# One encoder block on one core: load queues, load order, and PSUM banks rearranged from mLSTM to the last matmul

## The chip, the cores and the metric

The kernel runs on one core of one Trainium2 chip. The metric is the device time of one execution in microseconds (us). Five engines work side by side, each on its own instruction stream and in order: TensorE (PE, with its weight loads, PEld), VectorE (DVE), ScalarE (ACT), GpSimd (POOL) and SyncE (SP). A DMA is started by an instruction on SP or POOL; a waiting instruction holds up everything behind it on the same engine.

## The reference

The input is x, 1024 rows of 1024 float32 channels, and one layer of parameters.

- xn = rmsnorm(x). One matrix w_in projects it to mLSTM's queries, keys, values, output gate and 16 gate channels, to attention's queries, keys and values, and to two sets of merge gates ga, gb.
- mLSTM: four heads (key width 128, value width 256), in both directions, in chunks of 128 rows. For each chunk, scores are weighted with exp(D - m), with D from cumulated gates; a state C is carried from chunk to chunk. Both directions are added, normalized and gated: h_a.
- Differential attention: eight heads with two softmaxes each (width 64, rope on queries and keys), weights p0 - lam*p1, times values of width 128, normalized: h_b.
- Merge: y = sigmoid(ga)*(h_a @ p_a) + sigmoid(gb)*(h_b @ p_b); x1 = x + y @ w_o.
- ConvFFN: u = rmsnorm(x1) @ w_up (5632 channels), a 3-tap convolution along the rows in each channel with a bias, (gelu(g)*a) @ w_down, added to x1.

## The kernel before

Nearly every product is made of three TensorE matmuls (`mm3`, lines 111 to 113): each float32 operand is split into a rounded high part and a low part (`split`, line 80 on ACT, line 82 on DVE or, in four pieces, line 87 on POOL). A stationary weight block is loaded from DRAM as a raw tile of 128 x 1024 (`Weights.load`, line 207, tag `wraw`, NR = 1 buffer for the whole kernel), split into `whi` and `wlo` (four buffers each), and the raw tile is free again after both. A projection needs two such loads, called g = 0 and 1.

The program is written with pools of tiles. A planner that simulates the kernel with a cost model sets the order of instructions on each engine; semaphores are put where a tile is written, read or reused. `K.mark` (line 703) keeps weight splits behind a given activation.

- **mLSTM** (`mlstm`, lines 257 to 545). Eight x tiles are loaded, in two halves (`load_x`, line 281), normalized and transposed by PE into xn. Then come the projections of head 0 (`project`, with `wqk` and `wv`), the 16 gate channels and a long chain over rows of 36 partitions on ACT and DVE (lines 362 to 414), whose results go through DRAM (u_d, iw_d) and come back broadcast over 128 partitions (pm, qs, lines 448 and 457). `core(h)` turns pm into exp(pm + cT) in eight pieces on ACT (line 451), masks it on POOL (line 453) and multiplies it with the scores on DVE (line 455); qs is multiplied on POOL (line 458), kw on DVE (line 460). Then chunk products run on PE (lines 471 to 476), while `ogate(h)` and `project(h+1)` give PE the other work. At the end of `project`, ACT copies kt (line 322), and `finish(h)` transposes the head's result (line 508).
- **Attention** (`attention`, lines 548 to 890). Thirty-two steps (8 heads x 4 pairs of query blocks). A step has the scores and softmax of the next step (`soft`, lines 697 to 708), the transposes and products of this one (`av`, lines 728 and 746), the end of the last one (`tail2`: scale `og` on ACT, line 766; transposes, line 769; `oT`, line 771; store hb_d, line 772) and a `filler`: projections for a later head or merge gates. `qk_piece` makes the keys and queries of a later head; `qk_turn` transposes them and stores the keys in order with four small DMAs on SP (kst, line 682), on which the scores wait. Fillers start weight loads on SP (line 207); POOL makes their low parts (line 87). The rope tables cos and sin come on SP too (line 630), sin with one buffer that POOL reads. POOL also takes the power -0.5 for norms (line 230).
- **Merge** (`merge_ffn`, lines 893 to 998). The tags are `wk` (2 buffers), `B` (16), `acc` (8) and `A` (16). For p_a, the blocks that are not done in attention are multiplied while `load_hb` brings h_b (hraw, tag `wk`, line 916) and splits it; the gates come in as tgl (tag `wk`, line 939). Then p_b and w_o follow. The convolution's parameters cw and cb are read one float32 at a time from DRAM (lines 1017 and 1018) and used some 270 us later. PSUM is four single banks and two double ones here; before `Up.run` this pool is closed and one of eight single banks is opened.
- **Up** (lines 1001 to 1253) and **Down** (lines 1256 to 1420). w_up's product is done in a seven-product scheme for 22 column blocks, each followed by the convolution, gelu and stores h_d. Down does w_down in seven products n of NK = 11 blocks kk: for each, `make` loads a weight tile wd when n < 2 (line 1300, tag `B` for even and `A` for odd), then `prep` calls `act`, which requests the activations hr (line 1332, tag `acc`, two kk per load), and splits both. Three blocks are made ahead. One block is four row tiles of three matmuls.

## Time and profile before

| what | value |
|---|---|
| times of three runs | 2169.25, 2174.41 (median), 2174.93 us |
| the profiled execution's own time, and its span | 2177.57 and 2175.8 us |
| PE busy (11804 matmuls), weight loads | 2095.0 us, 1809.5 us |
| DVE, ACT, POOL busy | 1297.1, 971.5, 412.4 us |
| mean granted clock of PE | 0.984 |
| DMA moved, mean | 217.38 MB, 100 GB/s |

The stages lie about at 0 to 490 us (mLSTM), 490 to 1265 (attention), 1265 to 1500 (merge) and 1500 to 1946 (Up), and Down is the rest. A busy PE need not be PE at its peak: the granted clock of a stretch must be read beside it, where 1.00 is 2.4 GHz and 0.50 is 1.2 GHz. In a row of instructions the bracket at the end is the time that the engine stood idle before it and what it waited for.

### The profile page before, as it was taken

The page shows a single profiled execution, that of the slowest core. Times are in us where ns is not written, and L with a number is a line of the kernel's source. Part 1 is how long each engine was busy: PE and PEld are TensorE (multiplying, and loading weights), DVE is VectorE, ACT ScalarE, POOL GpSimd, SP SyncE. Part 2 cuts the span into 40 slices and gives each one's busy share as a digit, 9 for nine tenths or more (in the row PEclk, how much of TensorE's full clock was granted, in tenths as well). Part 3 has the DMA queues.
Part 4 walks back from the last instruction along what each step waited for, and adds up shares of the span by engine and source line. Part 5 has one row for each costly group of instructions (what it writes and reads, how often), then busy time and mean ns, then how long its engine had stood idle before and what let it go on. Part 6 is the DMA issues. An engine that isn't in the chain of part 4 may idle for free.

```text
span 2175.8 us, 30577 instructions
## 1 busy us (share of the span) xinstructions
PE 2095.0 (96%) x11804; PEld 1809.5 (83%) x11804; DVE 1297.1 (60%) x2110; ACT 971.5 (45%) x1837; POOL 412.4 (19%) x487
## 2 busy tenths in 40 slices
PE   7999999999999899999999999999999999979999
PEld 6878878898898898988988887898788888868887
DVE  4356343545585766848756424425877777778554
ACT  4343232234565555646655422205645444434443
POOL 0122101132341523414220000000121122120000
PEclk9999999999999999999999999999999999999999
DMA  4224221253322325133332385511232323266441
GB/s 127 39 84 123 67 60 49 68 136 59 100 59 54 84 56 93 53 82 75 78 99 78 127 180 182 160 45 78 87 112 84 121 87 116 91 243 242 139 136 46
DMA packets 210242, 217.38 MB, mean 100 GB/s; under 512 B 40841, under 2 KB 172969, under 8 KB 210097
## 3 DMA queue, kind: packets, MB, share of 16 engines
q1 hardware_dynamic: 202224, 187.58, 30.6%
q0 software_dynamic: 7872, 27.86, 3.8%
q8 instruction: 93, 1.52, 0.3%
q14 instruction: 53, 0.43, 0.1%
HBM read 149.82 MB, written 48.79 MB: 91 GB/s over the span
## 4 chain that ended last, share of the span: by engine, by line
PE 76%; DMA 8%; DVE 5%; ACT 4%; issue 4%; POOL 2%; SPq 1%; ACTq 0%; DVEq 0%; POOLq 0%
PE sm L112 12%; PE sm L113 12%; PE sm L111 12%; PE pj L111 8%; PE pj L113 8%; PE pj L112 8%; DMA wraw<-in_w_in_dram 4%; PE big L697 4%; PE pt L728 1%; DMA kst<-st 1%; PE cr L471 1%; PE po L111 1%; PE po L112 1%; PE po L113 1%; POOL wlo L87 1%
## 5 line engine op out<-in xcount | busy, mean ns | idle before, releaser
L111 PE MATMUL pj<-whi,xn 128*128 128x256 f32 x960 | 274.9, 286 | 1.2 <-ACT raw L624 0.5
L113 PE MATMUL pj<-whi,xn 128*128 128x256 f32 x960 | 274.3, 286 | 0.0
L112 PE MATMUL pj<-wlo,xn 128*128 128x256 f32 x960 | 273.8, 285 | 0.0
L111 PE MATMUL pj<-xn,whi 128*128 128x512 f32 x512 | 211.7, 415 | 3.8 <-ACT xn L252 3.1
L113 PE MATMUL pj<-xn,wlo 128*128 128x512 f32 x512 | 208.3, 407 | 0.0
L112 PE MATMUL pj<-xn,whi 128*128 128x512 f32 x512 | 207.9, 406 | 0.0
L80 ACT CAST whi<-wraw 128x1024 fp32r<-128x1024 f32 x88 | 92.3, 1049 | 226.7 <-DMA wraw<-in_w_in_dram 118.0
L111 PEld LDWEIGHTS pj<-whi,xn 128*128 128x128 f32 x960 | 182.7, 190 | 4.9 <-ACT raw L624 1.0
L112 PEld LDWEIGHTS pj<-wlo,xn 128*128 128x128 f32 x960 | 182.6, 190 | 1.9
L113 PEld LDWEIGHTS pj<-whi,xn 128*128 128x128 f32 x960 | 182.6, 190 | 1.4
L703 ACT ACTIVATE p<-big,smx 128x1024 f32<-128x1024 f32 x128 | 143.5, 1122 | 76.8 <-DVE smx L701 65.2
L701 DVE TENSOR_REDUCE smx<-big 128x1 f32<-128x1024 f32 x128 | 154.3, 1217 | 38.8 <-PE big L697 38.2
L82 DVE TENSOR_TENSOR wlo<-wraw,whi 128x1024 fp32r<-128x1024 f32 x54 | 67.2, 1244 | 181.9 <-ACT whi L80 181.9
L697 PE MATMUL big<-kst,qst 128*128 128x512 f32 x512 | 145.4, 405 | 12.3 <-DMA kst<-st 9.3
L1230 POOL TENSOR_TENSOR cv<-cv,cv 128x256 f32<-128x256 f32 x88 | 78.9, 923 | 355.9 <-ACT cv L1226 134.1
L87 POOL TENSOR_TENSOR wlo<-wraw,whi 128x256 fp32r<-128x256 f32 x136 | 112.2, 856 | 163.6 <-ACT whi L80 163.6
L113 PE MATMUL sm<-AS,ul 128*128 128x512 f32 x352 | 138.6, 397 | 0.9 <-DVE ul L82 0.9
L112 PE MATMUL sm<-AS,uh 128*128 128x512 f32 x352 | 138.6, 395 | 0.9 <-DVE AS L82 0.9
L111 PE MATMUL sm<-AS,uh 128*128 128x512 f32 x352 | 138.3, 395 | 0.4 <-ACT AS L80 0.4
L82 DVE TENSOR_TENSOR wTl<-pt,wTh 128x512 fp32r<-128x512 f32 x128 | 86.5, 685 | 81.1 <-ACT wTh L80 80.9
L111 PE MATMUL sm<-dh 128*128 128x512 f32 x308 | 120.0, 393 | 13.6 <-ACT dh L80 13.6
L111 PEld LDWEIGHTS pj<-xn,whi 128*128 128x128 f32 x512 | 98.6, 193 | 26.7 <-ACT xn L252 3.5
(303 smaller groups left out, 5287.7 us busy)
## 6 DMA issues: line engine op xcount, KB each, us to landing
ur<-in_w_up_dram SPq DMA_DIRECT2D x88, 256.0 KB, 3.4
wraw<-in_w_in_dram SPq DMA_DIRECT2D x40, 512.0 KB, 5.2
hr<-h_d SPq DMA_DIRECT2D x35, 512.0 KB, 6.3
kst<-st SPq DMA_DIRECT2D x128, 128.0 KB, 2.4
wraw<-in_w_in_dram SPq DMA_DIRECT2D x48, 256.0 KB, 4.7
h_d<-cv SPq DMA_DIRECT2D x22, 512.0 KB, 3.2
wd<-in_w_down_dram SPq DMA_DIRECT2D x22, 512.0 KB, 6.3
x<-in_x_dram SPq DMA_DIRECT2D x16, 512.0 KB, 4.6
```

What stands on the lines that cost most here:

```text
L80: self.nc.scalar.copy(hi, src)
L82: self.nc.vector.tensor_tensor(lo, src, hi.bitcast(F32), op=ALU.subtract)
L87: lo_eng.tensor_tensor(lo[:, t], src[:, t], hi[:, t].bitcast(F32), op=ALU.subtract)
L111: mm(ps, a[0], b[0], start=start, stop=False, skip_group_check=again)
L112: mm(ps, a[0], b[1], start=False, stop=False, skip_group_check=again)
L113: mm(ps, a[1], b[0], start=False, stop=stop, skip_group_check=again)
L471: T.matmul(nps[:, :MV + 1], pm[:, t], va[:, j, :], start=True, stop=i == 0)
L697: T.matmul(sps[c_][:, half * 512:half * 512 + 512], o.q[st.qp][:, c_, t], o.k[half][:, c_, s_, :], start=s_ == 0, stop=s_ == 1)
L701: V.tensor_reduce(sm[:, c_:c_ + 1], sp, op=ALU.max, axis=AX.X, negate=True)
L703: K.mark = A.activation(p_, sp, AF.Exp, bias=sm[:, c_:c_ + 1], accum_out=sm[:, 2 + c_:3 + c_]).ins
L728: T.transpose(pt[:, kk * 256 + j * P:kk * 256 + (j + 1) * P], st.w[j][:, kb * P:(kb + 1) * P], K.ident)
L1230: nc.gpsimd.tensor_tensor(a[:, t], a[:, t], g[:, t], op=ALU.mult)
```

## The change

1. Raw weight tiles alternate between two buffers in mLSTM (`rawp`: one of the pool wp, one of mLSTM's own pool).
2. The second half of x is requested after the first half is normalized, on POOL's queue.
3. exp(pm + cT): one DVE addition of 128 x 1024 and one ACT exponential take the place of eight ACT pieces; qs is multiplied on DVE.
4. In attention, from step 1 on, weight loads are issued by POOL (`ldq`), and sin by POOL throughout.
5. `tail2` keeps the scaling; the transposes, oT and the store become `tail3`, called inside the next `av` after its first yield.
6. Merge: PSUM is eight single banks from the start, and there is no second pool; gates for p_a are loaded straight into ya; the convolution's parameters are loaded as rows of 128 (craw, tag `wk`) and transposed by PE (`turn_conv`).
7. Down: `act` is called ahead of the weight load, and the first two hr tiles take tag `B`.

```diff
-    def wgran(self, loads, lo_eng=None):
...
     def load(self, g):
         K = self.K
-        self.raw = K.wp.tile([P, 1024], F32, tag="wraw", bufs=NR, name=K.nm("wraw"))
+        K.nraw += 1
+        self.raw = K.rawp[K.nraw % len(K.rawp)].tile([P, 1024], F32, tag="wraw", bufs=NR, name=K.nm("wraw"))
...
-            K.nc.sync.dma_start(self.raw.rearrange("p (k c) -> p k c", k=4)[:, :, off:off + n],
-                                s[g * 512:(g + 1) * 512].rearrange("(k p) c -> p k c", p=P))
+            (K.ldq or K.nc.sync).dma_start(self.raw.rearrange("p (k c) -> p k c", k=4)[:, :, off:off + n],
+                                           s[g * 512:(g + 1) * 512].rearrange("(k p) c -> p k c", p=P))
...
         K.psum(es, {"pj": 2, "cr": 4}, 1)
+        K.rawp = [K.wp, mp]
...
             if first:
-                xs0 = load_x(0)
+                xs0 = load_x(0, nc.sync)
             wqk = K.load_w([w_in[:, O_MQ + h * 128:O_MQ + h * 128 + 128], w_in[:, O_MK + h * 128:O_MK + h * 128 + 128]])
-            if first:
-                xs1 = load_x(1)
...
             if first:
                 norm(xs0, 0)
+                xs1 = load_x(1, G)
...
-                for j in range(8):
-                    t = slice(j * P, (j + 1) * P)
-                    A.activation(pm[:, t], pm[:, t], AF.Exp, bias=cT[:, j, rr:rr + 1])
+                V.tensor_tensor(ch(pm), ch(pm), bc(cT[:, :, rr:rr + 1], [P, 8, P]), op=ALU.add)
+                A.activation(pm, pm, AF.Exp)
...
-                G.tensor_tensor(qs, qT, qs, op=ALU.mult)
+                V.tensor_tensor(qs, qT, qs, op=ALU.mult)
...
-            for t_, d_ in zip((cos, sin), K.rope_d):
-                nc.sync.dma_start(t_, d_[bp * P:(bp + 1) * P, :])
+            for q_, t_, d_ in zip((nc.sync, G), (cos, sin), K.rope_d):
+                q_.dma_start(t_, d_[bp * P:(bp + 1) * P, :])
...
-        def av(st, hook):
+        def av(st, hook, hook0):
...
                 yield
+                if kp == 0 and hook0:
+                    hook0()
                 if kp < 2:
...
                 A.activation(st.og[:, t], po[:, t], AF.Copy, scale=inv[:, 6 + j:7 + j])
+
+        def tail3(st):
+            po = st.po
             for j in range(2):
...
+            if i == 1:
+                K.ldq = G
...
-            both(av(cur, (lambda: soft(o, nxt, 1)) if nxt else None), filler(h, 2 * qp))
+            both(av(cur, (lambda: soft(o, nxt, 1)) if nxt else None,
+                    (lambda: tail3(steps[i - 1])) if i else None), filler(h, 2 * qp))
...
+        K.ldq = None
...
-        K.psum(es, {"sm": 4})
+        K.psum(es, {"sm": 8}, 0)
...
+        craw = g4("craw", tag="wk")[:NFF * 2, :4 * P]
+        for t in range(4):
+            src = I["conv_w"][0][t, 0] if t < 3 else I["conv_b"][0]
+            nc.sync.dma_start(craw[:, t * P:(t + 1) * P], src.rearrange("(k p) -> k p", p=P))
+        conv = fp.tile([P, 3, 44], F32, tag="cw", name="cw"), fp.tile([P, 44], F32, tag="cb", name="cb")
+
+        def turn_conv():
+            ps = K.small()
+            for t in range(4):
+                T.transpose(ps[:, t * 44:t * 44 + 44], craw[:, t * P:(t + 1) * P], K.ident[:44, :44])
+            V.tensor_copy(conv[0].rearrange("p t k -> p (t k)"), ps[:, :132])
+            V.tensor_copy(conv[1], ps[:, 132:176])
...
-                    tg = g4("tgl", tag="wk")
+                    tg = g4("tgl", tag="wk") if gidx else ya[m]
...
                         if gidx == 0:
+                            if m == K.ny + 1 and half == 0:
+                                turn_conv()
...
-        up.norm0([g4("nxs", tag="wk") for _ in range(2)] + [g4("nxs", tag="B") for _ in range(2)], pair)
+        up.norm0([g4("nxs", tag="wk") for _ in range(2)] + [g4("nxs", tag="B") for _ in range(2)], lambda k: K.small())
...
-        es.close()
-        K.psum(es, {"sm": 8}, 0)
         up.run()
...
-        for t in range(3):
-            nc.sync.dma_start(self.cw[:, t, :], K.I["conv_w"][0][t, 0].rearrange("(k p) -> p k", p=P))
-        nc.sync.dma_start(self.cb, K.I["conv_b"][0].rearrange("(k p) -> p k", p=P))
+        self.cw, self.cb = conv
...
-        if kk % 2 == 0:
+        if kk % 2 == 0 and (n, kk) not in self.raw:
             (i, c), m = self.ORDER[n][0], min(2, self.NK - kk)
-            t = self.g4("hr", tag="acc")
+            t = self.g4("hr", tag="B" if n == 0 and kk < 4 else "acc")
...
         def make(n, kk):
+            self.act(n, kk)
             if n < 2:
                 self.load_w(kk * 2 + n)
```

## Rows read from the trace of the kernel before

**Rows 1.** PE's waits: engine, line, waited for: us in total, times, longest us
```profile
PE sm L111 <- ACT dh L80: 13.6, 1, 13.6
...
PE big L697 <- DMA kst<-st: 9.3, 5, 4.1
PE cr L508 <- ACT kt L322: 7.2, 2, 5.3
...
PE po L769 <- ACT og L766: 4.3, 2, 2.3
...
PE pj L111 <- ACT xn L252: 3.1, 1, 3.1
PE sm L111 <- ACT f L1074: 3.0, 1, 3.0
```

**Rows 2.** Stretches: us, busy us of PE, PEld, DVE, ACT, POOL, clock, DMA share, GB/s
```profile
97.00:136.00 39.00, 32.64 (x148) 26.05 (x147) 30.00 (x34) 16.86 (x40) 15.23 (x16) 0.87 0.39 117
278.00:290.00 12.00, 6.70 (x34) 5.94 (x34) 6.14 (x7) 2.51 (x4) 0.00 (x0) 0.72 0.59 100
655.00:668.00 13.00, 8.89 (x53) 8.39 (x52) 5.10 (x11) 6.44 (x16) 4.00 (x5) 0.74 0.47 100
748.00:760.00 12.00, 7.86 (x30) 6.10 (x29) 4.55 (x9) 6.11 (x15) 3.65 (x5) 0.72 0.56 120
935.00:945.00 10.00, 7.99 (x33) 6.05 (x32) 4.84 (x9) 4.29 (x12) 3.35 (x5) 0.83 0.33 95
1106.00:1116.00 10.00, 7.71 (x32) 5.91 (x31) 5.10 (x9) 4.62 (x10) 3.84 (x6) 0.83 0.35 83
1311.00:1328.00 17.00, 11.95 (x35) 8.48 (x34) 7.36 (x8) 5.03 (x5) 2.36 (x5) 0.70 0.57 185
1503.00:1515.00 12.00, 9.00 (x41) 7.10 (x40) 7.64 (x14) 7.92 (x14) 1.65 (x2) 0.86 0.23 88
1944.00:1966.00 22.00, 8.39 (x27) 6.33 (x26) 17.18 (x24) 8.90 (x13) 4.24 (x5) 0.69 1.02 393
2000.00:2050.00 50.00, 50.00 (x222) 41.42 (x221) 29.43 (x47) 21.27 (x38) 0.00 (x0) 1.00 0.29 91
```

**Rows 3.** ACT in order of time at the start: start us, us, instruction [idle before]
```profile
14.72 1.04 ACT L80 CAST whi<-wraw 128x1024 fp32r<-128x1024 f32 x1 [3.37 <-DMA wraw<-in_w_in_dram]
15.98 1.03 ACT L242 ACTIVATE big<-x 128x1024 f32<-128x1024 f32 x1 [0.22 <-DMA x<-in_x_dram]
```

**Rows 4.** ACT and DVE in order of time, 85 to 132 us
```profile
87.70 1.05 ACT L80 CAST whi<-wraw 128x1024 fp32r<-128x1024 f32 x1 [5.58 <-DMA wraw<-in_w_in_dram]
...
121.88 6.41 DVE L460 TENSOR_TENSOR kw<-kt,e1T 128x1024 f32<-128x1024 f32 x2 [4.32 <-ACT e1T L421]
```

**Rows 5.** ACT in order of time, 255 to 300 us
```profile
282.78 1.04 ACT L80 CAST whi<-wraw 128x1024 fp32r<-128x1024 f32 x1 [7.11 <-DMA wraw<-in_w_in_dram]
```

**Rows 6.** SP's issues in order of time, 640 to 664 us
```profile
654.51 0.94 SPq L207 DMA_DIRECT2D wraw<-in_w_in_dram  x2
655.54 2.56 SPq L682 DMA_DIRECT2D kst<-st  x4
```

**Rows 7.** SP's waits in attention, 495 to 1200 us
```profile
SPq L207 <- POOL wlo L87: 82.0, 26, 4.8
```

**Rows 8.** POOL by line: busy us, mean ns, idle before; triggers (all), powers (490 to 1250)
```profile
L448 POOL DMA_DIRECT2D pm<-u_d x8 | 4.6, 578 | 4.1 <-DVE dn L486 2.8 <-DMA u_d<-row 1.2
...
L230 POOL TENSOR_TENSOR inv<-inv,mhalf 128x2 f32<-128x2 f32 x31 | 23.6, 760 | 274.1 <-DVE inv L229 274.0
```

**Rows 9.** SP's issues in order of time, 1195 to 1330 us
```profile
1272.71 13.73 SPq L1017 DMA_DIRECT2D cw<-in_conv_w_dram  x3
...
1291.35 35.41 SPq L207 DMA_DIRECT2D wraw<-in_p_b_dram  x5
```

**Rows 10.** Chain that ended last, in order of time, 1940 to 1965 us
```profile
1946.06 0.02 issue
...
1947.94 11.02 DMA hr<-h_d
```

More of the change, by code (lines that the diff above doesn't have):

```diff
@@ L61, in __init__ @@
         self.gst, self.ng, self.ny = {}, 0, 0
+        self.rawp, self.nraw, self.ldq = [self.wp], 0, None
     def nm(self, s):
@@ L87, in split @@
             lo_eng.tensor_tensor(lo[:, t], src[:, t], hi[:, t].bitcast(F32), op=ALU.subtract)
-    def wgran(self, loads, lo_eng=None):
-        nc = self.nc
-        raw = self.wp.tile([P, 1024], F32, tag="wraw", bufs=NR, name=self.nm("wraw"))
-        for view, src in loads:
-            nc.sync.dma_start(view(raw), src)
-        hi = self.wp.tile([P, 1024], F32R, tag="whi", bufs=NH, name=self.nm("whi"))
-        lo = self.wp.tile([P, 1024], F32R, tag="wlo", bufs=NW, name=self.nm("wlo"))
-        self.split(hi, lo, raw, lo_eng)
-        return hi, lo
     def load_w(self, srcs, lo_eng=None):
@@ L274, in mlstm, with load_x @@
         xv = I["x"][0]
-        def load_x(half):
+        def load_x(half, eng):
             r = []
@@ L280, in load_x @@
                 t = mp.tile([P, 1024], F32, tag="r4", bufs=9, name=K.nm("x"))
-                nc.sync.dma_start(t, xv[blk * P:(blk + 1) * P, :])
+                eng.dma_start(t, xv[blk * P:(blk + 1) * P, :])
                 r.append(t)
@@ L545, in mlstm @@
             finish(h, hs, t1)
+        K.rawp = [K.wp]
 def attention(K, xn, hb_d):
@@ L890, in attention @@
         tail2(steps[-1])
+        tail3(steps[-1])
 def merge_ffn(K, ha_d, hb_d, out):
@@ L960, in merge_ffn @@
         nc.sync.dma_start(g2, I["norm2"][0].rearrange("(k p) -> p k", p=P))
-        pw = []
-        def pair(k):
-            if k % 2 == 0:
-                pw.append(K.big())
-            return pw[-1][:, k % 2 * 512:k % 2 * 512 + 512]
         def wo_piece(w, cg, b0):
@@ L984, in merge_ffn @@
         ws = [wo(2), wo(3)]
-        up = Up(K, g4, acc, g2, fp)
+        up = Up(K, g4, acc, g2, fp, conv)
         up.us = [up.load(0), up.load(1)]
@@ L1001, with __init__ @@
 class Up:
-    def __init__(self, K, g4, acc, g2, fp):
+    def __init__(self, K, g4, acc, g2, fp, conv):
         self.K, self.g4, self.acc, self.g2 = K, g4, acc, g2
@@ L1013, in __init__ @@
         nc = K.nc
-        self.cw = fp.tile([P, 3, 44], F32, tag="cw", name="cw")
-        self.cb = fp.tile([P, 44], F32, tag="cb", name="cb")
-        for t in range(3):
-            nc.sync.dma_start(self.cw[:, t, :], K.I["conv_w"][0][t, 0].rearrange("(k p) -> p k", p=P))
-        nc.sync.dma_start(self.cb, K.I["conv_b"][0].rearrange("(k p) -> p k", p=P))
+        self.cw, self.cb = conv
         self.x1_d = K.dr.tile([S, D], F32, tag="x1_d", name="x1_d")
@@ L1333, in act @@
                                      src.rearrange("(k p) t -> p k t", p=P))
-            self.raw[n] = t
-        return self.raw[n][:, kk % 2 * 512:kk % 2 * 512 + 512]
+            self.raw[n, kk] = t
+        return self.raw[n, kk // 2 * 2][:, kk % 2 * 512:kk % 2 * 512 + 512]
     def prep(self, n, kk):
```

## The prediction, made before the result was known

> **What bounds the kernel now.** First PE's busy time: 2095.0 of 2175.8 us. PE never stops for long, so a change that leaves PE's matmuls as they are can win back only two things: the time in which PE waits, and the time in which it runs at the low clock after a wait. So the second view is the list of PE's waits [rows 1]: the reader is to see that they are few and long (13.6 us once, 9.3 in five, 7.2 in two), and that each has a place. The third view takes a stretch around each place [rows 2] and gives two numbers: the length less PE's busy time is idle, and the mean clock c says how much of the stretch was granted 1.2 instead of 2.4 GHz: 2(1-c) of its length, since there are only these two levels. Work done then takes twice as long, so the clock costs at most (1-c) times the length; a part of the low stretch is the wait itself, so I take two thirds. Around 2000 us the clock is 1.00 and 222 matmuls fill 50 us: 0.225 us each at full pace.
>
> Idle plus clock, in us: 97 to 136: 6.4 + 3.4 = 9.8. 278 to 290: 5.3 + 2.2 = 7.5. 655 to 668: 4.1 + 2.3 = 6.4. 748 to 760: 4.1 + 2.2 = 6.3. 935 to 945: 2.0 + 1.1 = 3.1. 1106 to 1116: 2.3 + 1.1 = 3.4. 1311 to 1328: 5.1 + 3.4 = 8.5. 1503 to 1515: 3.0 + 1.1 = 4.1. 1944 to 1966 holds one kind of matmul, so it goes directly: 22 - 27 x 0.225 = 15.9. Outside these: 3.1 at the start and 1.9 (7.2 - 5.3) for the second of the L508 waits [rows 1]. The sum is 70 us. The change touches each of these places, so 70 us is what it can win from them.
>
> **Part by part.** *Start.* ACT runs in order; at 14 us it holds the weight cast until 14.72, then a square over x's second half until 17, and only then the first xn copy on which PE waits 3.1 us [rows 1, 3]. With that half of x asked for after the first norm, neither stands in the way. PE needs the second half only after the first half's products. Bounds: -3.1 to +1 (one square's length late); I take -2.5, near the wait's own size.
>
> *Second raw buffer.* ACT waited 5.6 us at 82 to 87.7 for a weight load that could start only when the one buffer was free; the gate rows come behind it on ACT, and their chain ends in both PE waits of 97 to 136 [rows 2, 4]. At 275.7 the same: 7.1 us of waiting ahead of the kt copy that PE's transposes need [rows 1, 5]. With two buffers the second load of a pair travels beside the first, so the chain starts up to 5.6 us earlier, against 6.4 us of idle in it. What is late next is pm on DVE, behind two kw's that took 6.41 us together beside POOL's work [rows 4]. Bounds: 0 to 9.8 for the first, 0 to 9.4 for the two L508 waits; I take -8 and -8, near the upper ends, because each wait names this load or what stands behind it.
>
> *exp and qs.* Eight ACT pieces become a DVE addition and one long exponential; DVE gets 16 operations in four heads. Priced by half of the kw pair, 3.2 us at worst, that is 51 us on an engine that is busy 30 of 39 us in the one stretch where it matters [rows 2, 4], and beside PE elsewhere. Bounds: -3.2 (one such operation shorter) to +6.4 (two longer); I take 0, since POOL loses the multiplications that ran beside the kw's.
>
> *Weight loads and sin on POOL.* SP stood 82 us, 26 times, at a weight load whose buffer POOL had not freed [rows 7]; at 654.51 the load goes out and the four kst stores right behind it [rows 6], and PE waits for these. That is the wait of 655 to 668, and 748 to 760 looks the same. On POOL the load follows the split that frees the buffer, and SP goes on to kst. Gain 0 to 12.7; I take -10 (kst can still stand behind a store of hb_d). The price: from step 1 on there are 42 weight triggers (4 in head 0, 6 in each of heads 1 to 5, 4 in head 6, 2 gates and 2 of p_a in head 7) and 32 of sin. A POOL trigger of 128 rows takes 0.58 us [rows 8]; a weight trigger has 512 pieces, so it costs from 0.58 to four times that, 2.3. That is 43 to 116 us of POOL in 760, where it now idles 274 us before the power `inv` alone [rows 8]. Beside other work it costs nothing; ahead of an `inv`, a late result. Bounds at PE -0 to +71 (31 x 2.3); I take +4, two late results of 2 us, near the low end since POOL idles 8.8 us before an average `inv`.
>
> Here the Trainium skill speaks against the change. "DMA: Bandwidth & Descriptors", section "Issuing engines are not separate DMA queues", says that DMAs of all issuing engines run on the same 16 DMA engines, and that spreading them saves only the sequencer's issue time. By that rule the 10 us would be nothing, and the sum -41. The trace differs in this: SP's 82 us are waits ahead of the issue, on a buffer, which the rule does not speak of [rows 7].
>
> *tail3.* PE waits 4.3 us in two places for the scaled og [rows 1], 6.5 us with the clock (935, 1106). Called after two groups of transposes and a piece of filler, the transposes come some 2 us later than the scaling. Bounds: -6.5 to +6.5 (oT now sits right ahead of the products in the same bank, and two waits of that size come up for it); I take -4.
>
> *Merge.* The parameter reads held SP from 1272.71 for 18.6 us, so p_b's weights were asked for at 1291.35 [rows 9]; ACT waited for them with the h_b casts behind, and PE at 1312 for these. Four reads of whole rows, and gates that no longer take `wk` buffers, remove both; `craw` holds one of the two `wk` until m = 5. Bounds 0 to -8.5; -7.5.
>
> *One set of banks.* PE waited 3.0 us for the last reader of a bank of the old pool [rows 1]. With eight free banks it waits for none; next is the last low part of the same operand, about when PE gets there. 0 to -4.1; -3.5.
>
> *Down.* The first hr was issued at 1947.94, after Up's last product (1946.06) had ended, because `acc` came free only then, and took 11.0 us [rows 10]. In tag `B`, and ahead of the weights, it goes out when Up's early `B` tiles come free. What is late next is kk = 4, still in `acc`: PE reaches it after 4 x 12 x 0.225 = 10.8 us, at 1956.9; hr lands at 1958.96 and its cast, half as wide as one of 1.04 [rows 5], takes about 0.6, so 2.7 us of wait and 1.7 of clock stay. 15.9 - 4.4 = 11.5. Bounds: -15.9 if hr lands sooner; -4.9 if the weight tiles that hr pushes out of the early `B` slots come a whole such load, 11.0 us, late.
>
> **Sum.** -2.5 - 8 - 8 - 10 + 4 - 4 - 7.5 - 3.5 - 11.5 = -51. On the profiled execution's own 2177.57 that is 2126.6; this execution is 3.2 above the median of three, 2174.4, so the time is 2123.4, said as 2124.
>
> **The rivals.** *Attention's move gives nothing* (16%): kst stays behind SP's waits for hb_d, or the transfers, not SP, are the limit. For it: the DMA share is 0.47 and 0.56 in the two stretches [rows 2]. Against: kst goes out right behind the load [rows 6]. The 10 us go: 2133. The page of the Trainium skill named above would have it so. *Down and merge only move* (14%): the DMA share is 1.02 at 1944 to 1966 [rows 2], so the first blocks come earlier and later ones late, and the planner gives `craw`'s buffer back late. For it: that share. Against: at 2000 to 2050 the share is 0.29, so a late block is soon made up. Of 11.5 + 7.5 = 19 us 5 stay: 2137. *All waits go* (8%): 2174.4 - 70 + 4 = 2108. *New waits eat the gain* (6%): every stream is ordered anew, and waits of 1 to 4 us as in rows 1 come up elsewhere; within 6.5 us of before. *POOL decides* (8%), the slower one: each of 31 `inv` comes behind a 512-piece trigger of 2.3 us and PE waits for it in each step: +71 for the +4, and 10 of gain gone: 2174.4 - 51 + 67 + 10 = 2200. It decides from 55 / 31 = 1.8 us a step. For it: triggers of that kind were never on POOL. Against: its idle time.
>
> **How the numbers follow.** The forecast has 48%; its own range is 2110 to 2140. With the two rivals that stay faster and the one beyond it, 86% are faster by over 0.3% (6.5 us, about what a measurement of this kernel tells from no change), 6% the same, 8% slower. The range 2100 to 2156 holds the forecast and all faster cases with gains from 18 to 74 us; left out are the last two cases and the tails.
>
> **What would show it.** Right: no PE wait for dh at Up's end over 4 us; SP's waits at a weight load gone from attention and none of PE for kst over 2 us; ACT's wait before the gate rows under 2 us; no PE wait at the first hbh products; POOL's weight triggers under 1.5 us. Wrong: new PE waits behind POOL's `inv` or weight splits, a wait in Down at kk = 2 to 6 of the old size, or waits for wTl or oT in every step. Half of the gain gone with no such wait would mean that the clock's share was misjudged.

## The result, and the profile after

The changed kernel took 2151.0 us (median of 4 runs, 2144.8 to 2153.5); the kernel before took 2174.6 in the same comparison. The ratio is 0.9893, with an interval of [0.9866, 0.9920]: 23.6 us faster, where 51 were forecast. The profiled execution took 2153.5 us, the longest of the four, and its span is 2151.8. One of e7's four executions below took 11697.5 us; its median is of all four, its ratio of the other three, 2145.2 to 2146.7. First the busy times:

```profile
PE 2081.1 (97%) x11808; PEld 1803.0 (84%) x11808; DVE 1328.1 (62%) x2128; ACT 961.8 (45%) x1781; POOL 450.4 (21%) x557
```

PE is 13.9 us less busy. Now PE's waits, the view that answers to [rows 1]:

```profile
PE cr L242 <- DVE x L236: 13.7, 2, 12.3
PE pt L719 <- DVE wTl L83: 8.4, 6, 3.7
PE sm L101 <- ACT dh L81: 7.3, 1, 7.3
PE pt L662 <- DVE wTl L83: 5.1, 3, 2.9
PE cr L461 <- DVE dn L476: 3.9, 1, 3.9
...
PE sm L101 <- ACT f L1078: 2.3, 1, 2.3
```

Of the waits of [rows 1], those for kst, kt, xn and og (line 766 before) are gone; so is that for hbh in merge, which rows 2 showed as a stretch. The wait for dh at the end of Up is half as long. In their place stand a first product at 12.31 us instead of 9.07, and waits for wTl all through attention (16.1 us in 12 places; 4.6 before). A wait for f is there as before, at another place. So is one for the masked scores pm, 3.9 us: it is told by dn, which ended 0.06 us after pm (rows further down), and the kernel before had it too:

```profile
PE cr L471 <- DVE pm L455: 3.8, 1, 3.8
```

The same stretches as in [rows 2], moved where their work has moved (length, busy us of PE, PEld, DVE, ACT, POOL, clock, DMA share, GB/s):

```profile
97.00:136.00 39.00, 33.87 (x165) 26.93 (x163) 30.64 (x42) 13.66 (x20) 9.39 (x14) 0.96 0.38 116
278.00:290.00 12.00, 12.00 (x65) 10.16 (x64) 11.01 (x12) 1.71 (x3) 1.52 (x1) 1.00 0.53 175
631.00:640.00 9.00, 5.26 (x27) 5.09 (x26) 8.82 (x14) 5.00 (x11) 5.63 (x8) 0.67 0.32 76
1311.00:1328.00 17.00, 17.00 (x76) 13.94 (x75) 9.87 (x13) 3.74 (x6) 0.53 (x1) 1.00 0.38 115
1503.00:1515.00 12.00, 9.51 (x38) 6.32 (x36) 12.00 (x20) 10.47 (x20) 0.00 (x0) 1.00 0.09 25
1935.00:1957.00 22.00, 14.68 (x55) 11.57 (x54) 19.24 (x28) 8.07 (x13) 3.65 (x5) 0.77 1.04 404
```

278 to 290 and 1311 to 1328 are full now. 97 to 136 still has 5.1 us of idle, 1503 to 1515 has 2.5 us, Down's stretch 7.3, and 631 to 640, a place that [rows 2] does not have, has 3.7 us and a clock of 0.67.

To see which part of the program gained, take the starts of four products that every version has: the last one that transposes hs (the end of the mLSTM), the first of scores (kst, qst), the first of merge that runs in a bank sm, and the last of all. Two of them, as the view of one line gives them (count, shortest/median/longest ns, first to last start):

```profile
L498 PE MATMUL cr<-ident,hs x64: 270/272/273, 184.5 to 436.9; 128*128 128x128 f32 x64
L688 PE MATMUL big<-kst,qst x512: 387/394/632, 471.0 to 1197.4; 128*128 128x512 f32 x171
```

| stretch, us | before | before, 2nd profile | after | change | forecast |
|---|---|---|---|---|---|
| to the end of the mLSTM | 446.1 | 446.5 | 436.9 | -9.2 | -18.5 |
| entry of attention (to the first scores) | 30.7 | 30.7 | 34.1 | +3.4 | (with attention) |
| attention (to merge's first product) | 787.8 | 787.5 | 787.5 | -0.3 | -10 |
| merge, Up and Down | 906.7 | 904.8 | 889.0 | -17.7 | -22.5 |
| sum | 2171.3 | 2169.5 | 2147.5 | -23.8 | -51 |

The kernel before repeats these to 2 us (its second profile is e18 below). The changed one doesn't in attention, as the experiments show, and its profile here, with 821.6 us for entry and attention, is among the longest there.

### The profile page after: what moved, and what is told of

It reads as the page before. It is cut to its first block, busy times and chain, and to the rows that moved or that the text cites. A ratio compares the mean times of both kernels' runs of the same rounds, so it can differ in the third digit from the quotient of the medians.

```text
span 2151.8 us, 30492 instructions
## 1 busy us (share of the span) xinstructions
PE 2081.1 (97%) x11808; PEld 1803.0 (84%) x11808; DVE 1328.1 (62%) x2128; ACT 961.8 (45%) x1781; POOL 450.4 (21%) x557
## 3 DMA queue, kind: packets, MB, share of 16 engines
q1 hardware_dynamic: 152492, 165.55, 25.9%
## 4 chain that ended last, share of the span: by engine, by line
PE 56%; DMA 2%; DVE 2%; ACT 1%; issue 1%; SPq 0%; POOL 0%; ACTq 0%; DVEq 0%
PE sm L101 13%; PE sm L102 13%; PE sm L103 13%; PE pj L101 3%; PE pj L102 3%; PE pj L103 3%; PE big L688 2%; PE pt L719 1%; DMA kst<-st 1%; PE po L101 1%; PE po L102 1%; PE po L103 1%; DMA hr<-h_d 0%; DMA wd<-in_w_down_dram 0%; PE big L101 0%
## 5 line engine op out<-in xcount | busy, mean ns | idle before, releaser
L102 PE MATMUL sm<-dl,dh 128*128 128x512 f32 x308 | 120.3, 392 | 0.0
```

What stands on the lines that cost most here:

```text
L102: mm(ps, a[0], b[1], start=False, stop=False, skip_group_check=again)
```

## The experiments

All are the changed kernel with one edit, except e12, e16, e17 (several) and e18. Times are medians; the kernel before ran on the same chip each time. The table has what the verdicts rest on, in us; "entry + attention" runs from the end of the mLSTM to merge's first product.

| run | time | ratio to before [interval] | first product | end of mLSTM | entry | entry + attention | merge to end |
|---|---|---|---|---|---|---|---|
| before | 2174.6 | | 9.1 | 446.1 | 30.7 | 818.5 | 906.7 |
| after | 2151.0 | 0.9893 [0.9866, 0.9920] | 12.3 | 436.9 | 34.1 | 821.6 | 889.0 |
| e1 sin on SP | 2156.8 | 0.9933 [0.9918, 0.9949] | 12.5 | 437.4 | 30.7 | 824.2 | 888.9 |
| e2 weights on SP | 2156.2 | 0.9926 [0.9913, 0.9940] | 12.8 | 437.7 | 34.4 | 822.7 | 891.0 |
| e3 both on SP | 2150.8 | 0.9899 [0.9884, 0.9914] | 12.6 | 437.1 | 30.9 | 815.4 | 889.5 |
| e4 tail3 in tail2 | 2151.4 | 0.9904 [0.9886, 0.9923] | 12.3 | 436.2 | 34.2 | 814.5 | 889.2 |
| e5 sin earlier | 2151.9 | 0.9904 [0.9885, 0.9923] | 12.3 | 437.4 | 34.2 | 813.9 | 890.5 |
| e6 x held back | 2149.3 | 0.9886 [0.9871, 0.9902] | 9.0 | 436.2 | 33.8 | 815.6 | 889.6 |
| e7 four hr in B | 2146.0 | 0.9876 [0.9861, 0.9890] | 12.5 | 436.9 | 34.1 | 816.9 | 885.4 |
| e8 Down as before | 2158.8 | 0.9941 [0.9929, 0.9954] | 12.5 | 436.1 | 34.6 | 816.6 | 897.9 |
| e9 one raw buffer | 2149.5 | 0.9891 [0.9876, 0.9905] | 12.2 | 437.6 | 34.3 | 818.5 | 890.9 |
| e10 exp and qs as before | 2143.5 | 0.9861 [0.9841, 0.9881] | 12.3 | 431.2 | 34.4 | 813.4 | 889.0 |
| e11 pm's rows on SP | 2147.1 | 0.9874 [0.9859, 0.9889] | 12.3 | 438.5 | 33.6 | 813.8 | 889.4 |
| e12 e6 + e7 + e11 | 2149.0 | 0.9880 [0.9862, 0.9897] | 8.9 | 435.6 | 34.6 | 822.0 | 886.9 |
| e13 exp as before | 2145.8 | 0.9872 [0.9852, 0.9891] | 12.4 | 433.4 | 34.3 | 815.7 | 889.6 |
| e14 qs as before | 2146.4 | 0.9868 [0.9852, 0.9884] | 12.3 | 434.8 | 34.7 | 813.6 | 890.4 |
| e15 e9 + e10 | 2159.7 | 0.9937 [0.9920, 0.9955] | 12.2 | 448.1 | 34.6 | 812.8 | 889.4 |
| e16 e6 + e7 + e10 | 2138.2 | 0.9836 [0.9819, 0.9853] | 9.4 | 430.7 | 34.4 | 818.9 | 887.1 |
| e17 e16 + e3 | 2137.2 | 0.9829 [0.9816, 0.9843] | 8.8 | 428.8 | 30.6 | 819.7 | 883.9 |

Entry and attention together scatter between 812.8 and 822.0 in the twelve profiles whose code there is that of the changed kernel (after, e6 to e16); the mean is 816.6. The other columns repeat to 1 to 3 us where their code is the same (merge to end is 885.4, 886.9, 887.1 and 883.9 in e7, e12, e16 and e17).

What scatters can be read from the whole stretch, entry and attention, before, after and in e10 (columns as above). The numbers of products are the same but for one at the edge:

```profile
446.10:1264.60 818.50, 793.15 (x5346) 716.97 (x5345) 516.93 (x803) 451.46 (x957) 234.99 (x254) 0.99 0.34 85
436.90:1258.50 821.60, 791.68 (x5347) 716.46 (x5346) 537.62 (x803) 453.24 (x957) 288.71 (x331) 0.99 0.35 84
431.20:1244.60 813.40, 786.93 (x5347) 712.70 (x5346) 531.39 (x803) 453.55 (x957) 289.06 (x331) 1.00 0.35 85
```

Length less busy time is PE's idle time: 25.4, 29.9 and 26.5 us; over the twelve profiles it is 25.2 to 30.6, in the mean 27.4. The rest of the scatter is busy time for these products, from 786.6 us in e11 to 791.8 in e16, and it goes with the granted clock, 1.00 there and 0.99 here. So the change did not lower PE's idle time in attention at all: other waits took the place of those that went.

### Attention's queues: e1 to e5, e17, e18

```diff
 # e1: sin on SP                  e2: weight loads on SP
-zip((nc.sync, G), (cos, sin))    -K.ldq = G
+zip((nc.sync, nc.sync), ...)     +K.ldq = None        # e3: both
 # e4: tail3(steps[i - 1]) right behind tail2(steps[i - 1])
 # e5: next block's sin asked for behind the two products that free its buffer
```

> The changed kernel with one edit: sin is requested from SP again, as cos is; weight loads stay on GpSimd. In the changed kernel's trace five DVE operations on two SBUF operands that take 0.68 us elsewhere took 3.7 to 4.0 us, each time when a sin trigger on GpSimd is followed within 27 ns by the four low-part operations of a weight; two more took 2.5 and 3.7 us in such a run. PE then waits for wTl, oT or st. Theory (triggers on GpSimd hold DVE out of its operand reads for the whole run that follows): DVE operations held by over 1 us in attention fall from 8 to at most 2, PE's waits for wTl in attention from 16 us to under 7, and 8 to 14 us come back: 2137 to 2143. Rival 1 (the weight triggers are what holds DVE): holds stay, 2148 to 2154. Rival 2 (sin's wait for its buffer stands on SP ahead of kst again): holds go, PE waits for kst come back, 2143 to 2150.

> The changed kernel with one edit: weight loads go out on SP throughout, sin stays on GpSimd. Theory of e1 (a trigger right ahead of a run of low-part operations holds DVE): sin triggers still stand there, so some holds over 1 us stay (3 to 8), and SP's waits for weight buffers put kst late again (PE waits for kst 5 to 9 us): 2150 to 2160. Rival 1 (weight triggers do the harm): holds gone, 2138 to 2145. Rival 3 (GpSimd's queue does no harm, attention lost its gain to tail3's new place): within 3 us of 2151.

> The changed kernel with weight loads and sin both on SP, as before; all other parts stay. If the whole move of loads to GpSimd gave nothing net, as a comparison of the two traces by stretches says (attention 64 us of PE time over full pace before, 68 after), this is within 4 us of 2151; no DVE operation held over 1 us, PE waits for kst 7 to 10 us. If the move is worth the 10 us of the prediction and something else cost them: 2160 or more. If the move itself costs: 2140 or less.

> The changed kernel with tail3 called right behind tail2 again. The prediction gave tail3 -4 us, with -6.5 to +6.5 as bounds. If that holds: PE waits for og at the scaled transposes return (2 or more, 2 us each) and the time is 2154 to 2158. If the products that follow oT in the same bank are what PE now waits for (waits for oT 2.0 us and part of those for wTl): 2145 to 2149. If tail3 does nothing: within 2 us of 2151.

> The changed kernel with one edit: GpSimd asks for the next block's sin right behind its two multiplications that free the buffer, instead of at the next block. The same triggers stay on GpSimd, but the weight's four low-part operations then seldom follow one at once. Theory (a trigger with a run of low-part operations behind it holds DVE for the run): DVE operations held by over 1 us in attention fall from 8 to at most 3, PE's waits for wTl from 16 us to under 8; PE's time over full pace in attention from 66 to 54 to 60 us, the time 2139 to 2147. Rival (any order of triggers costs the same, since weights land late for ACT's casts): attention stays at 64 us or more, 2148 to 2154.

Here is what the theory of e1 speaks of, from the changed kernel: DVE, GpSimd and PE in order of time near 630 us (start, us, instruction):

```profile
629.51 3.72 DVE L637 TENSOR_TENSOR raw<-raw,cos 128x512 f32<-128x512 f32 x1
...
629.24 0.62 POOL L621 DMA_DIRECT2D sin<-rope  x1
629.88 2.79 POOL L88 TENSOR_TENSOR wlo<-wraw,whi 128x256 fp32r<-128x256 f32 x4
632.96 1.51 POOL L198 DMA_DIRECT2D wraw<-in_w_in_dram  x2 [0.29 <-POOL wlo L88]
...
635.10 0.45 PE L719 MATMUL pt<-ident,p 128*128 128x128 f32 x1 [3.74 <-DVE wTl L83]
```

DVE's product, 0.68 us elsewhere, is under way when the sin trigger ends and the four low-part operations begin 21 ns later; it ends 0.56 us after the last of them. wTl stands behind it on DVE, and PE waits 3.74 us. One DVE line, shortest/median/longest in 32, before, after, in e1, e2 and e3:

```profile
L649 DVE TENSOR_TENSOR raw<-raw,qss x32: 676/693/1254, 461.4 to 1106.4; 128x512 f32<-128x512 f32 x32
```
```profile
L640 DVE TENSOR_TENSOR raw<-raw,qss x32: 675/692/3957, 453.7 to 1101.3; 128x512 f32<-128x512 f32 x32
```
```profile
L640 DVE TENSOR_TENSOR raw<-raw,qss x32: 672/691/1218, 452.6 to 1093.2; 128x512 f32<-128x512 f32 x32
```
```profile
L640 DVE TENSOR_TENSOR raw<-raw,qss x32: 665/683/3935, 454.7 to 1092.2; 128x512 f32<-128x512 f32 x32
```
```profile
L640 DVE TENSOR_TENSOR raw<-raw,qss x32: 673/692/1256, 452.5 to 1096.4; 128x512 f32<-128x512 f32 x32
```

Over all DVE lines, operations held by more than 1 us were 8 after (21.5 us together), 2 in e1 (1.2 to 1.7 us), 4 in e2 (2.4 to 3.3 us), 0 in e3, e17 and in both profiles of before. So the holds of over 2 us go with the sin trigger, not the weight's. The Trainium skill, "SBUF — State Buffer", section "SBUF: two separate sides", says that GpSimd and a DVE operation with two SBUF inputs take turns on one port pair, each for a whole instruction. The half microsecond of lines before (1254 - 693 ns) agrees with one GpSimd instruction of about 0.7 us; 3.0 us here (3.72 - 0.68), until all four had ended, is more than that rule gives.

But e1's gain didn't come. The holds went, PE's waits for wTl fell from 16.1 to 7.9 us, kst hardly came back (2.1 us), and the time was 2156.8, which neither the theory nor a rival had. PE waited elsewhere, 9.1 us for tg where it had been 2.0. In one such place ACT, in order, stood 3.1 us at a weight that GpSimd had asked for at 1097.36, and tg stood behind it:

```profile
1105.64 0.80 PE L101 MATMUL pj<-xn,whi 128*128 128x512 f32 x1 [3.94 <-ACT tg L154]
```

That is no price of GpSimd's queue as such: in all of attention, ACT waits for weights of w_in 26.3 us after, 37.5 in e1, 20.1 in e2, and with both loads on SP 34.7 (e3) and 34.4 (before). In e2 as in e1 one half of the move makes the time 5 us worse (each of their twelve executions took longer than all four of the changed kernel); why stays open. Without both (e3) it is the same as with both.

e2 met its time and its four holds, but not the other half of its theory. SP again stood 69.6 us in 26 waits at weight loads (82.0 in [rows 7]), and PE did not wait for kst at all. Where only one of the two loads is on SP, or none, PE hardly waits for kst (0 to 3.5 us in all); only where sin and weights are both on SP it does, 7.2 us in e3, and in the fastest version, e17, 9.9, most of it here:

```profile
PE big L691 <- DMA kst<-st: 9.0, 2, 5.0
PE po L768 <- ACT og L762: 3.9, 2, 2.0
```

The second row is news for tail3: the waits for og that it was to remove [rows 1] are there in e17 and e3 (3.4 us), with tail3 in place, and not in e4, without it. They went with the loads' move; tail3 does nothing that could be seen (e4 2151.4, within the 2 us of its last case). e5 moved the request and five holds of over 1 us stayed: its expectation failed, since the planner put low parts right behind the trigger again.

> e16 with weight loads and sin in attention asked for by SP as before. In twelve profiles of kernels with the changed attention, from its first score product to merge's first product it took 778 to 788 us, mean 782; with both loads on SP (e3) 784.5; before 787.8 (one profile). If the move of these loads is worth nothing net: within 3 us of 2138. If it is worth the 10 us of the prediction and something else lost it: 2144 to 2150. If it costs: 2135 or less. PE's waits for kst return (7 to 10 us), DVE operations held over 1 us go.

> The kernel before once more, for a second profile of its attention: 787.8 us from the first score product to merge's first product in the first one. If single profiles of it scatter as those of the changed one do: 780 to 792. Its five waits for kst should be there again (9 us in all), and no DVE operation held over 1 us.

2137.2 against 2138.2: the move is worth nothing net in the fastest version too. On GpSimd the waits for kst and og go, PE waits for wTl 11.7 us (e16) instead of 4.3 (e17), and attention's entry takes 34 us, wherever sin is on GpSimd, instead of 31: there GpSimd asks for the first sin at 445.90 us and then stands 4.10 us for it. The kernel before gave 787.5 us and 9.2 us of kst waits in its second profile, as foreseen.

### The start: e6

```diff
+                if after:
+                    G.tensor_copy(t[:, :1], after[b4][:, :1])
                 eng.dma_start(t, xv[blk * P:(blk + 1) * P, :])
...
-                xs1 = load_x(1, G)
+                xs1 = load_x(1, G, xs0)
```

> The changed kernel with one edit: a copy of one column of each normed first-half block into the tile for the second half of x makes its read wait for the norm, so that it can't go out ahead of the first half's reads. In the changed kernel GpSimd asked for it at 1.68 us, SP for the first half at 1.92. Theory (the two halves and the weights share the transfers, so the first block of x lands at 7.4 us instead of 6.2): the first matmul is at 9.1 to 9.5 us instead of 12.31, and 2.5 to 5 us come back, less 0 to 2 for a second half that is late: 2146 to 2149. Rival (what is won at the start is waited for again at the gate rows' chain, whose end sets PE at 128 us): first matmul as early, but PE's time over full pace up to 140 us no lower than 20 us, time within 2 us of 2151.

The changed kernel's start: GpSimd, SP, ACT and PE in order of time.

```profile
1.68 2.30 POOL L273 DMA_DIRECT2D x<-in_x_dram  x4
1.92 2.39 SPq L273 DMA_DIRECT2D x<-in_x_dram  x4
...
7.42 1.03 ACT L233 ACTIVATE big<-x 128x1024 f32<-128x1024 f32 x1 [5.03 <-DMA x<-in_x_dram]
...
12.31 1.12 PE L242 MATMUL cr<-ident,x 128*128 128x128 f32 x4 [12.31 <-DVE x L236]
```

The second half of x stands behind the norm in the program's text, but the planner puts on GpSimd what it thinks ready, and nothing held it: it went out ahead of the first half, which landed at 7.42 instead of 6.25 us, and block by block later. Held back, the first product is at 9.01 us. Only 0.7 of these 3.3 us are left at the end of the mLSTM (436.9 to 436.2): the wait for the second pm grew from 3.9 to 5.4 us, and PE waits 2.2 us for xn again (3.1 in [rows 1]). So theory and rival are both half right; the time, 2149.3, is within the scatter of attention.

### Down: e7, e8

```diff
 # e7                                             # e8
-tag="B" if n == 0 and kk < 4 else "acc"          tag="acc", and act() behind load_w()
+tag="B" if n == 0 and kk < 8 else "acc"
```

> The changed kernel with Down's first four activation loads in B instead of two. In the changed kernel PE reached kk = 4 at 1938.96 and waited 7.5 us for the first load in acc, asked for at 1935.60 and landed 10 us later. Theory (the buffer decides when this load goes out): the wait at kk = 4 goes or falls under 2 us and Down's 10 us of time over full pace to 3 to 6: 2144 to 2148. Rival (the transfers decide: DMA share 0.99 through this stretch, and two more tiles of B push weights back): PE waits as long for a weight or at kk = 8, 2149 to 2155.

> The changed kernel with Down as before: all activation loads in acc and behind their weights. If Down's edit is worth what the two traces show (16.3 us over full pace before, 10.0 after), the wait of 13 us at the end of Up returns and the time is 2155 to 2160. If Down's load order only moves the wait: within 2 us of 2151. If the prediction's 11.5 was right and something else in this stretch lost 5 us: 2161 to 2164.

The chain that ended last in the changed kernel, in order of time, answers to [rows 10]:

```profile
1926.10 9.41 DMA wd<-in_w_down_dram
...
1935.60 10.37 DMA hr<-h_d
...
1945.99 0.63 ACT dh L81
...
1946.67 0.80 PE sm L101
```

PE's waits there, in e8 and in e7:

```profile
PE sm L101 <- ACT dh L81: 14.6, 1, 14.6
```
```profile
PE sm L103 <- DVE dl L83: 3.1, 1, 3.1
```

From merge to the end e8 took 897.9, the changed kernel 889.0 and e7 885.4: Down's edit is worth 8.9 us, and two more loads in B another 3.6 (2 to 5, by the repeats of this column). The buffer decides, as e7's theory said; 3.1 us of a later wait stay.

### The gate chain and the kt waits: e9 to e16

```diff
 # e9                        # e13: the exponential as before
-K.rawp = [K.wp, mp]         -V.tensor_tensor(ch(pm), ch(pm), bc(cT[...]), op=ALU.add)
+K.rawp = [K.wp]             -A.activation(pm, pm, AF.Exp)
                             +for j in range(8): A.activation(..., AF.Exp, bias=cT[:, j, rr:rr + 1])
 # e11: pm's rows by SP      # e14: qs as before
-G.dma_start(pm, ...)        -V.tensor_tensor(qs, qT, qs, op=ALU.mult)
+nc.sync.dma_start(pm, ...)  +G.tensor_tensor(qs, qT, qs, op=ALU.mult)    # e10: e13 + e14
```

> The changed kernel with one raw weight buffer in the mLSTM, as before, instead of two. The prediction gave the second buffer -8 at the gate chain (97 to 136) and -8 at the two waits for kt. The two traces show PE's time over full pace in the mLSTM after 140 us at 22.3 before and 19.7 after, the waits for kt gone, and a wait of 4.1 us for pm still there at 128.6. Theory (the buffer is worth what stood on ACT: kt's waits, and 4 to 5 us up to 140 us): two waits for kt of 3 to 7 us return, and the time is 2157 to 2163. If it is worth the 16 us of the prediction: 2165 or more. If what ACT and PE wait for is set elsewhere: within 2 us of 2151.

> The changed kernel with pm's exponential in eight ACT pieces with a bias and q times its scale on GpSimd, as before. The prediction gave this edit 0. In the changed trace the first kw pair took 3.25 us instead of 6.41, since GpSimd no longer multiplied beside it, but pm of the second direction came no earlier. If 0 holds: the kw pair takes over 5 us again, the wait at 125 to 129 us is within 1 us of 4.1, and the time within 2 us of 2151. If the edit carries the gain of the gate chain: first pm product 3 us later, 2153 to 2157. If DVE's extra operations cost more than they give: 2147 or less.

> The changed kernel with one edit: pm's broadcast rows are asked for by SP instead of GpSimd. In the changed trace the second direction's row went out at 120.83 us, behind the mask of the first on GpSimd (119.55 to 120.83), and PE waited 4.1 us at 128.6 for this pm. Theory (the place in GpSimd's queue is what is late after the second raw buffer, so the -8 of the prediction came out as -4): the second row goes out 4 to 7 us sooner, the wait falls under 1.5 us, with the low clock behind it 4 to 6 us come back: 2145 to 2148. Rival (DVE's line of kw, qs and low parts sets pm's time anyway): the wait stays at 3 us or more, within 2 us of 2151.

> The changed kernel with three edits together: the second half of x held back until the norm, pm's rows asked for by SP, Down's first four activation loads in B. By the single profiles: start 12.3 to 9.1 us (-3.2), the wait for pm of 4 to 6 us with its clock (-4 if SP's queue is free), Down 10.0 to 5.0 us over full pace (-5): -12 in all, 2136 to 2142. If the start's gain is only waited for later at the gate rows: 2142 to 2146.

> The changed kernel with only the exponential as before (eight ACT pieces with a bias, no DVE addition); q times its scale stays on DVE. With both as before (e10) the time was 2143.5 and the start of attention 5.4 us earlier than in the changed kernel, and 59 instead of 26 other products stood on PE between the first products of the two directions. Theory A (the DVE addition, and with it the planner's earlier place for the second direction's products, is what costs): wait at 125 to 130 us under 2.5 us, attention starts at 465 to 467, 2142 to 2146. Theory B (q's multiplication on DVE costs): wait of 4 us stays, attention starts at 470 to 472, 2148 to 2152.

> The changed kernel with only q's multiplication on GpSimd as before; the exponential stays one addition on DVE and one long ACT operation. Theory A: the wait for the second direction's pm at 125 to 130 us stays at 3 us or more, attention starts at 469 to 472, 2147 to 2152. Theory B: attention starts at 465 to 467, 2142 to 2146.

> The changed kernel with the exponential and q's multiplication as before and one raw weight buffer as before: the mLSTM then differs from the kernel before only in when the second half of x is asked for. In e9 (one buffer, new exponential) the waits for kt did not come back; in e10 (two buffers, old exponential) they were gone too. Theory (either edit alone removes these waits, so their gains don't add; the second buffer is worth some 14 us where the exponential is old): the waits for kt of 5.3 and 2 us return, attention starts at 477 to 481 and the time is 2154 to 2160. Rival (neither does it; the waits went with another edit or a new order): no wait for kt over 1 us, attention starts at 466 to 470, 2143 to 2148.

> The changed kernel with the exponential and q's multiplication as before, the second half of x held back until the norm, and Down's first four activation loads in B. From the single edits' profiles: e10 -5.4 at the start of attention, the start -3.2 where PE doesn't wait for it again at the gate rows (e6 kept 1.0 of it), Down -5: 2151 - 5.4 - 1 to 3.2 - 5 = 2137 to 2140. If the runs' own spread of attention (58 to 66 us over full pace with the same code there) falls badly: up to 2145.

e9 was a surprise: with one buffer the waits for kt stay away (0.6 us) and the time is the same. e10 was another: without the edit priced at 0 the time is 7.5 us less, 5.7 of them at the end of the mLSTM; the rest is attention's scatter. e15 joins them: with the old exponential and one buffer the waits for kt are back, 6.5 of the 7.2 us before, and the mLSTM ends at 448.1; the second buffer alone brings it to 431.2, the new exponential alone to 437.6, both to 436.9. PE's waits from 90 to 440 us in e15, and the same in e10:

```profile
PE cr L499 <- ACT kt L313: 6.5, 2, 5.1
PE cr L462 <- DVE pm L446: 3.5, 1, 3.5
PE cr L410 <- DVE row L370: 2.2, 1, 2.2
```
```profile
PE cr L462 <- DVE pm L446: 2.2, 2, 2.0
```

Why the new exponential costs where there are two buffers is seen in PE's order. The two first products with pm, one for each direction, DVE's operation that makes the second pm, in the changed kernel, and the stretch between the products (columns as above):

```profile
124.27 0.70 PE L461 MATMUL cr<-va,pm 128*128 128x257 f32 x2 [0.99 <-DVE pm L445]
131.39 1.21 DVE L445 TENSOR_TENSOR pm<-big,pm 128x1024 f32<-128x1024 f32 x1
132.75 1.20 PE L461 MATMUL cr<-va,pm 128*128 128x257 f32 x2 [3.91 <-DVE dn L476]
...
124.25:132.70 8.45, 4.57 (x30) 4.12 (x30) 6.22 (x8) 2.34 (x3) 1.24 (x2) 0.98 0.63 238
```

And in e10:

```profile
126.20 0.70 PE L462 MATMUL cr<-va,pm 128*128 128x257 f32 x2 [2.00 <-DVE pm L446]
134.54 0.67 PE L462 MATMUL cr<-va,pm 128*128 128x257 f32 x2 [0.20 <-DVE pm L446]
...
126.20:134.50 8.30, 8.13 (x63) 7.82 (x63) 2.05 (x5) 4.25 (x14) 3.45 (x2) 1.00 0.67 226
```

The second direction's pm comes 8.2 to 8.4 us after the first in both. In e10 the planner put 59 other products between them (63 less 4), in the changed kernel 26 (30 less 4): PE's order is fixed ahead of time, and it stands still for 3.91 us with work behind it. By the first product that transposes hs, at 184.5 us after and 180.4 in e10, 4.1 of the 5.7 us are there.

e11 asked for the second row 1.2 us sooner (119.60 instead of 120.83) and PE's wait grew to 5.12: its theory fell, the row wasn't it. That its time, 2147.1, lies where the theory had it is luck: its mLSTM ends later (438.5), its attention was short (813.8). e13 wins 3.5 of the 5.7 us (433.4), e14 2.1 (434.8), hardly more than this column's repeats. So most of the cost is the exponential's, which is theory A, though not in its numbers: e13 still waits 2.6 us there and starts attention at 467.7, and e14's time, 2146.4, is below what was said. e16 met its expectation; e12, without e10, did not, as its wait for pm stayed (5.1 us) and its attention was one of the two slowest of the twelve.

Why the new edit too removes the waits for kt (e9) can be read from the traces of e15 and e9, near the weight whose cast stands ahead of kt's copy on ACT. The first of the two loads in this place, in e15 and in e9, seen by its cast on ACT:

```profile
276.32 1.05 ACT L81 CAST whi<-wraw 128x1024 fp32r<-128x1024 f32 x1 [8.25 <-DMA wraw<-in_w_in_dram]
268.31 1.05 ACT L81 CAST whi<-wraw 128x1024 fp32r<-128x1024 f32 x1 [3.77 <-DMA wraw<-in_w_in_dram]
```

SP asked for this load at 266.78 in e15 and at 263.25 in e9, so it took 9.5 and 5.1 us. In e15 four broadcast reads of pm's and qs's rows go out on GpSimd right beside it, at 264.90 to 266.59, because they stand behind q's multiplication there, which waits 11.72 us for qT. In e9 that multiplication is on DVE: the reads go out at 249.02 to 250.67 and have landed before the load starts. The 4.5 us between the two loads are the 4.5 by which kt's longest wait fell (5.1 to 0.6). e13 and e14, with two buffers, show it of the reads alone: with q's multiplication on DVE they start at 245.07, with it on GpSimd at 260.26. Still it is a reading of traces; no run has one buffer and only this multiplication moved.

## Why the prediction was wrong

The sign and most places were right, and 51 was twice too much. 2151.0 lies in the range 2100 to 2156, but outside the forecast's own 2110 to 2140. By its steps, each against the runs:

- **Start, -2.5: wrong, the step "asked for after the first norm".** It took the order of the program's text for the order on the queue, which the planner writes. The first product came 3.2 us later, and by e15 (448.1, with the mLSTM otherwise as before, 446.1) that is +2.0 at the mLSTM's end; by e6 and by e16 against e10 it is 0.7 and 0.5, so little more than repeats. Held back as meant (e6), PE still waits 2.2 us for xn, so most of the -2.5 was not there to be had either.
- **Second raw buffer, -8 and -8: right where the exponential is old, by e15 and e10:** 448.1 - 431.2 = 16.9, of it 8.2 up to the first transposes of hs (188.6 to 180.4) and 8.7 behind them. ACT's waits of [rows 4, 5], 5.6 and 7.2 us in e15, are 0 and 0.3 us in e10. Beside the new exponential the same buffer gives 0.7 (e9, 437.6 to 436.9).
- **exp and qs, 0: wrong, mis-sized inside its bounds of -3.2 to +6.4.** It cost 436.9 - 431.2 = 5.7 us, and DVE's kw pair even got shorter (3.25 us for 6.41), but PE's order was written anew, with fewer products ahead of the second pm; why the planner did so no run shows. The sum also took the terms to add up. They don't: the edit alone (e9, -10.5) removes the waits that the buffer alone (e10) removes, and both together give 11.2 of 27.4 us.
- **Attention, -10 + 4 - 4: wrong, the step "Beside other work it costs nothing; ahead of an `inv`, a late result".** kst's wait went, but not for the reason given alone: in e2 SP stands at the weight loads nearly as before and PE doesn't wait for kst. The trigger's own time was right too, 0.77 us, under the 1.5 named as a sign. But the price shows on DVE, held for up to 3.3 us by what follows a trigger, in 16.1 us of PE waits for wTl instead of 4.6, and in an entry 3 us longer; PE's idle time in this stretch is no lower than before (25.4 and 25.9 us before, 27.4 in the mean of twelve). And -4 for tail3 was credited to the wrong edit. Entry and attention came out at +3.1 in this execution and at -1.9 in the mean of twelve (818.5 to 816.6). The rival "Attention's move gives nothing" has the right effect for a reason that it didn't name. The Trainium skill's rule that the prediction cites ("DMA: Bandwidth & Descriptors", section "Issuing engines are not separate DMA queues") has this effect too, but the kst waits that come and go show that the order of issue did matter.
- **Merge and banks, -7.5 - 3.5: near as a sum, 906.7 - 897.9 (e8) = 8.8 of 11, but by two errors that cancel.** From merge's first product to the first of w_o it takes 143.7 us before and 133.4 after (e8 too):

```profile
1264.60:1408.30 143.70, 138.65 (x579) 110.42 (x578) 62.33 (x76) 31.27 (x37) 9.67 (x18) 0.96 0.62 166
1258.50:1391.90 133.40, 133.40 (x584) 108.53 (x583) 62.26 (x77) 31.44 (x37) 7.94 (x15) 1.00 0.57 183
```

  That is -10.3, beyond the bound of -8.5: the idle 5.1 us of [rows 2] and the whole clock term (1 - 0.70) x 17 = 5.1, of which the prediction took two thirds. Behind it nothing was won: from w_o's first product to Up's last it is 537.3 us before (535.8 in the second profile) and 537.7 in e8. So the step that failed is "With eight free banks it waits for none": the 3.0 us are gone, but PE now waits 1.6 us for a norm at 1462 and 2.3 us at 1466 for a bank that ACT's f still reads. No run tries the banks alone.
- **Down, -11.5: right in kind, 8.9.** It named kk = 4, in `acc`, as late next, and so it was. It said that PE gets there 10.8 us after Up's last product; it took 5.2 (1934.1 to 1939.3), since the planner had run 25 of the 48 products before that. So the wait is 7.3 us, not 2.7.

Together: +2.0 - 16.9 + 5.7 + 3.1 - 8.8 - 8.9 = -23.8, the difference of the two profiles. Most of what is missing is in three steps: attention (13 us; 8 by the mean of twelve), the exponential (6) and the start (3 to 4.5). In all three an edit was costed on the engine that it loads or frees. At the start and at the exponential the order that the planner would write from it was taken to be the old one; in attention the engine beside it, DVE, was left out.

## What to carry to other kernels

Where a planner writes the order, a load's place in the text is no place in a queue: what must go later needs a dependency that says so. Cost a trigger on GpSimd also on DVE, by what stands right behind it on GpSimd, and judge such a move by PE's idle time in the whole stage, not by the one wait that goes. Two edits that remove the same wait are tried apart and together before their gains are added; here the fastest version, 2137 to 2138 us, leaves one of them out.

## What the runs showed that was not expected

- A DVE operation on two SBUF operands that is under way when GpSimd goes from a DMA trigger straight (21 to 27 ns) into four two-input operations took 3.7 to 4.0 us instead of 0.69, in the changed kernel five times; once, at 710.71 us, it took 0.69 in the same place, and what decides is not shown. Beside the same four operations without a trigger ahead it took 1.2 us.
- Executions of one kernel scatter by 2 to 16 us (e5: 2144.3 to 2160.1), and in the profiles of the changed kernels attention alone by 9 (812.8 to 822.0 us, entry included), while two profiles of the kernel before agree within 0.3 there (818.5 and 818.2). In attention one pair of profiles proves no edit of under 9 us.
